# A decoder layer on one core: VectorE's part of the modulation as row sums over transposed weights, with one more quarter of the FFN's shift and scale given to VectorE

## The chip, the cores and the metric

The kernel runs on one core of a Trainium2 chip. The metric is the device time of one execution in microseconds. Three runs of the kernel before took 1273.33, 1273.87 and 1276.59 us; the median is 1273.87.

The engines are named as in the profile: TensorE (PE, with PEld for its weight loads), VectorE (DVE), ScalarE (ACT), GpSimd (POOL) and SyncE (SP), whose queue issues nearly all loads.

## The reference, cut to what matters

The layer takes 256 tokens of width 2048 in float32, and one conditioning vector c.

```
mod = silu(c) @ w_ada + b_ada                      # w_ada: 2048 x 12288
shift_a, scale_a, gate_a, shift_f, scale_f, gate_f = split(mod, 6)      # 2048 each
h = rms_norm(x, g_attn_pre) * (1 + scale_a) + shift_a
proj = h @ w_in                                    # 2048 x 5456
mixed = concat(diff_attention(proj), indexed_sparse_attention(proj)) @ w_o
x = x + gate_a * rms_norm(mixed, g_attn_post)
h = rms_norm(x, g_ffn_pre) * (1 + scale_f) + shift_f
ff = (silu(h @ w_gate) * (h @ w_up)) @ w_down      # inner width 5632
out = x + gate_f * rms_norm(ff, g_ffn_post)
```

The change concerns the first line alone: 2048 x 12288 products of a vector with a matrix, 96 MB of weights that are each read once.

## The kernel before, in words

**Large products.** Every weight block of 1 MB is loaded into one of five `raw` buffers (`RAW`), split exactly into two parts by ScalarE (`whi`, L168) and VectorE (`wlo`, L169), and multiplied in three matmuls of 128x512 (`mm3`, L178, L181, L182). The parts have three buffers each (`WB`).

**The order of the stages.** The projection `w_in` runs in five passes over groups of 1, 1, 2, 4 and 8 K tiles (`GROUPS`), so that the modulation of a later group can be made while an earlier one is multiplied. In the last pass the blocks of columns come in an order of their own, and after each block one step of attention work is taken (`attn_step`). Then come the output projection in two halves of its columns, with a step of attention after each block of the first half, and the feed-forward in three parts. Its first blocks run over half of the rows while the rest of the modulation is made.

**The modulation.** It is a list of units of 1 MB, in order of use (`units`). `ada_step` takes the next one; its load is issued up to two units ahead (`AHEAD`) into the same `raw` buffers, and a unit can end with a closing step (`finish`) that is taken with the next one. In the last projection pass one unit is taken with each block, or two with every fourth (`RATE`); in the output projection one with each block (`side`); in the first part of the feed-forward two (`FRATE`).

Two engines share the units. On TensorE (`on_pe`) a unit is four K tiles of 512 columns, each multiplied by a column of silu(c), and the four tiles go to four groups of columns of the array (L225). On VectorE a unit is four multiply-adds of 128x512 into `aacc` (L233): the weights times silu(c) as a column, with the sum over the partitions left to the end. There shift and scale close with small products with a column of ones (L286) on VectorE's side and with `sel` (L282) on TensorE's. A gate closes with a product with `ones` (L301) that leaves the same row on every partition.

- The attention's shift and scale are all on TensorE (`A_DVE` is empty).
- The attention's gate: blocks 0 and 1 on TensorE, 2 and 3 on VectorE (`GA_DVE`).
- The FFN's shift and scale: four quarters of eight units. Quarter 2 is on VectorE (`F_DVE`), the others on TensorE.
- The FFN's gate: all four blocks on VectorE, made during the feed-forward.

**Who sets the order.** The kernel is written against a planner (`schedule_with_timeline_sim=True`) that orders each engine's queue before the run by estimated times, with the written order as priority, and places waits and buffers. So instructions stand in the trace in another order than in the code. [...]

**Places.** `xx`, a 32 KB buffer per partition under the tag `bigB`, holds x and its transposed copy, later the attention's output (`mixT`) and the FFN's activations (`gT`). `late_rows` (L122) loads gains and biases as rows, and `to_cols` turns them into columns.

Of the kernel before, what the change touches and what calls it, by code (L numbers as in the profile page):

```python
# [24 lines left out]
T = 2  # L25
# [13 lines left out]
GROUPS = (1, 1, 2, 4, 8)  # L39
GA_DVE = (2, 3)  # L40
F_DVE = (2,)
A_DVE = ()
RATE = (1, 1, 1, 2)
ATT = 1
FRATE = 2
RAW = 5
# [10 lines left out]
def layer(ctx, tc, x, c, positions, w_ada, b_ada, g_attn_pre, g_attn_post, g_ffn_pre,  # L57
# [26 lines left out]
    # ---- constants  # L84
# [20 lines left out]
    # ---- vectors, brought to columns  # L105
# [6 lines left out]
    xx = big.tile([P, 2, 4096], F32, tag="bigB", name="xx")  # L112
    xs = xx[:, 0, :].rearrange("p (t d) -> p t d", t=T)
    xT = xx[:, 1, :].rearrange("p (k q) -> p k q", k=KT)
# [4 lines left out]
    R2 = wp.tile([49, P], F32, tag="hf", name="rows2", bufs=2)  # L119
# [64 lines left out]
    # ---- adaLN modulation  # L184
# [6 lines left out]
    def ada_block(col0s, n, on_pe, finish, brow=None):  # L191
# [8 lines left out]
        def new_acc(b):  # L200
            st["acc", b] = wp.tile([P, 512], F32, tag="aacc", name=nm("aacc"), bufs=2)

        def load(b, u):
            if u == 0 and brow is not None and (b == 0 or not on_pe):
                new_acc(b)
                if not on_pe:
                    POOL.memset(st["acc", b], 0.0)
                SP.dma_start(st["acc", b][0:1], brow)
            raw = wp.tile([P, 2048], F32, tag="raw", name=nm("raw"), bufs=RAW)
            st[b, u] = raw.rearrange("p (k n) -> p k n", n=n)  # L210
            SP.dma_start(st[b, u], ada_w[u * kk * P:(u + 1) * kk * P, col0s[b]:col0s[b] + n]  # L211
                         .rearrange("(k p) n -> p k n", p=P))

        def use(b, u):
            if u == 0 and b == 0 and on_pe:
                st["ps"] = adp.tile([P, 512], F32, tag="ad", name=nm("ad"))
            if u == 0 and brow is None and not on_pe:
                new_acc(b)
            for i in range(kk):
                k = u * kk + i  # L220
                w = st[b, u][:, i, :]
                if on_pe:
                    j = k % 4
                    extra = brow is not None and j == 0
                    PE.matmul(st["ps"][32 * j:32 * j + 32, :n], lhsT=c33[:, k, 1 - b:33 - b], rhs=w,  # L225
                              start=(b == 0 and k < 4), stop=(b == nb - 1 and k >= 12 and not extra),
                              tile_position=(0, 32 * j))
                    continue
                acc = st["acc", b][:, :n]
                if k == 0 and brow is None:  # L230
                    DVE.tensor_scalar(acc, w, csil[:, 0:1], None, op0=ALU.mult)
                else:
                    DVE.scalar_tensor_tensor(acc, w, csil[:, k:k + 1], acc, op0=ALU.mult, op1=ALU.add)  # L233
            if u == nu - 1 and b == nb - 1:
                if on_pe:
                    if brow is None:
                        new_acc(0)
                    acc = st["acc", 0]
                    if brow is not None:
                        PE.matmul(st["ps"][0:32, :n], lhsT=ident[0:1, 0:32], rhs=acc[0:1, :n],  # L240
                                  start=False, stop=True, tile_position=(0, 0))
                    ACT.activation(acc[:, :n], st["ps"][:, :n], AF.Copy)
                    after.append(lambda: finish([acc]))
                else:
                    after.append(lambda: finish([st["acc", b] for b in range(nb)]))
# [28 lines left out]
    # shift and scale as columns: shift, and gain*(1+scale)  # L274
    def ada_cols(dst, chunk, bcol, g, col, n, on_pe):
        m, k0 = n // P, col // P

        def finish(accs):
            ps = tr_bank()
            for i in range(m):  # L280
                if len(accs) == 1:
                    PE.matmul(ps[:, 2 * i:2 * i + 2], lhsT=accs[0][:, i * P:(i + 1) * P], rhs=sel,  # L282
                              start=True, stop=True)
                else:
                    for b in range(2):
                        PE.matmul(ps[:, 2 * i + b:2 * i + b + 1], lhsT=accs[b][:, i * P:(i + 1) * P],  # L286
                                  rhs=ones[:, 0:1], start=True, stop=True)
            d = dst[:, :, k0:k0 + m]
            DVE.tensor_tensor(d, ps[:, :2 * m].rearrange("p (m b) -> p b m", b=2),
                              bcol.rearrange("p (b k) -> p b k", b=2)[:, :, k0:k0 + m], op=ALU.add)  # L290
            DVE.scalar_tensor_tensor(d[:, 1], d[:, 1], 1.0, g[:, k0:k0 + m], op0=ALU.add, op1=ALU.mult)

        ada_block([chunk * D + col, (chunk + 1) * D + col], n, on_pe, finish)

    # gate times the post gain, the same row on every partition
    def ada_gate(G, chunk, col, on_pe):
        c0 = chunk * D + col

        def finish(accs):
            ps = tr_bank()  # L300
            PE.matmul(ps, lhsT=ones, rhs=accs[0], start=True, stop=True)  # L301
            DVE.tensor_tensor(G[:, col:col + 512], ps, G[:, col:col + 512], op=ALU.mult)

        ada_block([c0], 512, on_pe, finish, b_ada[0:1, c0:c0 + 512])

    # ---- first norm, transposed
    ssx = ct([P, T], "ssx")
    rx = ct([P, T], "rx")
    for t in range(T):
        ACT.activation(xx[:, 1, 2048 * t:2048 * t + 2048], xs[:, t], AF.Square, accum_out=ssx[:, t:t + 1])  # L310
# [11 lines left out]
    def make_h(H, src, mod, k, qs=slice(0, S), lk=None, on_act=True):  # L322
        """A K tile of gain*(1+scale)*x + shift, split in two; the work shared by ACT and DVE."""
# [18 lines left out]
    def group_h(gi, k0, nk):  # L342
        H = pp.tile([P, 2, max(GROUPS[gi % 2::2]), S], F32R, tag=f"h{gi % 2}", name=nm("h"))
        for k in range(nk):
            make_h(H, xT[:, k0 + k, :], modA, k0 + k, lk=k)
        Hs[gi] = H
# [21 lines left out]
    # ---- attention parts; keys of token tile 0: [0:128], of tile 1: [128:384]  # L368
# [19 lines left out]
    def to_T(dst_cols, copy_eng=None):  # L388
        """Transposes of [tokens, 128] column blocks, side by side in one bank."""
# [8 lines left out]
    def idx_pairs(p0):  # L398
        """Stages for the four indexer heads of two 128-column blocks."""
# [30 lines left out]
    def attn_step(admit=1):  # L430
        """Moves every job in flight by one stage, the oldest first, and admits new ones."""
# [552 lines left out]
```

## Time and profile before

| | before |
|---|---|
| median of three runs | 1273.87 us |
| span of the profiled execution | 1272.5 us |
| fastest run | 1273.33 us |
| TensorE busy | 1233.9 us (97%) |
| VectorE busy | 774.3 us (61%) |
| ScalarE busy | 560.9 us (44%) |
| mean DMA rate | 244 GB/s |
| mean granted TensorE clock | 0.993 |

The page gives the profiled execution by its span, from its first instruction to its last. The fastest run shown lies 0.8 us above that and the median 1.4 us. Busy times are sums over an engine's instructions; TensorE's matmuls overlap, so a busy share near 1 says that it rarely waits, not that each matmul is at its shortest.

### The profile page before, as it was taken

The numbers are of one execution on the slowest core, as the hardware profiler recorded it, in microseconds if no ns is written. First come the engines' busy times: TensorE is split into PE (matmuls) and PEld (weight loads), VectorE is DVE, ScalarE is ACT, GpSimd is POOL, SyncE is SP. The second block draws the span as 40 slices with busy tenths as digits, with TensorE's granted clock in tenths as the row PEclk, the third lists the DMA queues.
The fourth block names the chain that finished last, engine by engine and source line by source line (L and its number), as shares of the span: only waits on it lengthen the run. The fifth ranks groups of instructions, "written<-read, shape, count | busy, mean of one in ns | idle before, by whom it ended". The sixth has DMA issues, their size and how long they took to land.

```text
span 1272.5 us, 15272 instructions
## 1 busy us (share of the span) xinstructions
PE 1233.9 (97%) x5938; PEld 950.3 (75%) x5938; DVE 774.3 (61%) x1160; ACT 560.9 (44%) x806; POOL 21.4 (2%) x55
## 2 busy tenths in 40 slices
PE   4999999999999999899999999999999999999996
PEld 3666666777666786688887888888888888888885
DVE  3576455898598683758867545754455454445565
ACT  4733333345345543764444444444444334444442
POOL 1000000000000000200000000000000000000000
PEclk8999999999999999999999999999999999999998
DMA  9999997978687487858878656766556555565541
GB/s 307 339 343 327 347 381 278 314 263 321 211 285 268 142 329 289 306 167 286 282 264 290 200 193 222 251 227 198 176 189 199 190 188 190 194 198 182 184 164 66
DMA packets 160090, 310.13 MB, mean 244 GB/s; under 512 B 5785, under 2 KB 19978, under 8 KB 158738
## 3 DMA queue, kind: packets, MB, share of 16 engines
q1 hardware_dynamic: 159938, 309.14, 70.7%
q8 instruction: 46, 0.75, 0.2%
q14 instruction: 26, 0.21, 0.0%
q10 hardware_dynamic: 80, 0.02, 0.0%
HBM read 307.05 MB, written 2.10 MB: 243 GB/s over the span
## 4 chain that ended last, share of the span: by engine, by line
PE 88%; DMA 4%; DVE 4%; issue 1%; ACT 1%; SPq 1%; POOL 0%; DVEq 0%; POOLq 0%; ACTq 0%
PE mm L181 26%; PE mm L178 26%; PE mm L182 25%; PE ad L225 5%; DMA raw<-in_w_ada_dram 4%; DVE aacc L233 2%; DVE wlo L169 1%; PE tr L474 1%; PE tr L411 1%; PE tr L918 1%; PE tr L830 1%; SPq L211 1%; PE tr L392 1%; PE tr L301 0%; PE tr L282 0%
## 5 line engine op out<-in xcount | busy, mean ns | idle before, releaser
L169 DVE TENSOR_TENSOR wlo<-raw,whi 128x1024 fp32r<-128x1024 f32 (+1 forms) x383 | 462.3, 1212 | 338.6 <-ACT whi L168 337.7
L168 ACT ACTIVATE whi<-raw 128x1024 fp32r<-128x1024 f32 (+1 forms) x383 | 400.3, 1050 | 522.4 <-PE mm L182 458.1
L181 PE MATMUL mm<-wlo,h 128*128 128x512 f32 (+1 forms) x1056 | 416.8, 395 | 1.9 <-DVE wlo L169 1.9
L182 PE MATMUL mm<-whi,h 128*128 128x512 f32 (+1 forms) x1056 | 409.9, 389 | 0.2 <-DVE h L335 0.2
L178 PE MATMUL mm<-whi,h 128*128 128x512 f32 (+1 forms) x1056 | 381.4, 394 | 2.4 <-ACT h L330 1.4
L181 PEld LDWEIGHTS mm<-wlo,h 128*128 128x128 f32 x1056 | 198.9, 188 | 62.5 <-issue 9.5
L178 PEld LDWEIGHTS mm<-whi,h 128*128 128x128 f32 x1056 | 196.8, 188 | 63.2 <-issue 13.6
L182 PEld LDWEIGHTS mm<-whi,h 128*128 128x128 f32 x1056 | 198.3, 188 | 42.5 <-issue 3.0
L181 PE MATMUL mm<-wlo,gT 128*128 128x512 f32 x348 | 135.8, 390 | 0.0
L182 PE MATMUL mm<-whi,gT 128*128 128x512 f32 x348 | 135.4, 389 | 0.0
L178 PE MATMUL mm<-whi,gT 128*128 128x512 f32 x348 | 123.0, 390 | 0.0
L233 DVE SCALAR_TENSOR_TENSOR aacc<-raw,csil,aacc 128x512 f32<-128x512 f32 x126 | 94.1, 746 | 23.8 <-DMA raw<-in_w_ada_dram 22.5
L225 PE MATMUL ad<-raw,c 128*32 128x512 f32 (+2 forms) x640 | 79.6, 537 | 9.9 <-DMA raw<-in_w_ada_dram 9.9
L733 DVE TENSOR_TENSOR PR<-mm,PR 128x512 f32<-128x512 f32 (+1 forms) x88 | 57.1, 669 | 41.2 <-PE mm L182 41.0
L182 PEld LDWEIGHTS mm<-whi,gT 128*128 128x128 f32 x348 | 65.3, 188 | 13.8 <-issue 0.2
L181 PEld LDWEIGHTS mm<-wlo,gT 128*128 128x128 f32 x348 | 65.3, 188 | 13.7 <-issue 0.2
L178 PEld LDWEIGHTS mm<-whi,gT 128*128 128x128 f32 x348 | 65.3, 188 | 13.4
L181 PE MATMUL mm<-wlo,mixT 128*128 128x512 f32 x124 | 49.1, 397 | 0.0
L178 PE MATMUL mm<-whi,mixT 128*128 128x512 f32 x124 | 47.5, 400 | 0.6 <-ACT mixT L587 0.6
L182 PE MATMUL mm<-whi,mixT 128*128 128x512 f32 x124 | 46.4, 399 | 0.0
L225 PEld LDWEIGHTS ad<-raw,c 128*32 128x32 f32 x640 | 17.6, 116 | 36.4 <-issue 31.3
L181 PEld LDWEIGHTS mm<-wlo,mixT 128*128 128x128 f32 x124 | 23.3, 188 | 7.8 <-issue 2.5
(195 smaller groups left out, 678.8 us busy)
## 6 DMA issues: line engine op xcount, KB each, us to landing
raw<-in_w_ada_dram SPq DMA_DIRECT2D x96, 1024.0 KB, 7.1
raw<-in_w_gate_dram SPq DMA_DIRECT2D x44, 1024.0 KB, 5.2
raw<-in_w_up_dram SPq DMA_DIRECT2D x44, 1024.0 KB, 5.1
raw<-in_w_down_dram SPq DMA_DIRECT2D x44, 1024.0 KB, 5.2
raw<-in_w_in_dram SPq DMA_DIRECT2D x39, 1024.0 KB, 6.9
raw<-in_w_o_dram SPq DMA_DIRECT2D x16, 1024.0 KB, 5.0
xx<-in_x_dram SPq DMA_DIRECT2D x2, 1024.0 KB
x<-in_x_dram SPq DMA_DIRECT2D x2, 1024.0 KB, 4.7
```

Source lines behind the costliest of these rows:

```text
L168: ACT.activation(hv, src, AF.Copy)
L169: DVE.tensor_tensor(lv, src, hv.bitcast(F32), op=ALU.subtract)
L178: i = PE.matmul(ps, lhsT=hi, rhs=whi, start=start, stop=False)
L181: PE.matmul(ps, lhsT=hi, rhs=wlo, start=False, stop=False)
L182: PE.matmul(ps, lhsT=lo, rhs=whi, start=False, stop=stop)
L211: SP.dma_start(st[b, u], ada_w[u * kk * P:(u + 1) * kk * P, col0s[b]:col0s[b] + n] .rearrange("(k p) n -> p k n", p=P))
L225: PE.matmul(st["ps"][32 * j:32 * j + 32, :n], lhsT=c33[:, k, 1 - b:33 - b], rhs=w, start=(b == 0 and k < 4), stop=(b == nb - 1 and k >= 12 ...
L233: DVE.scalar_tensor_tensor(acc, w, csil[:, k:k + 1], acc, op0=ALU.mult, op1=ALU.add)
L392: PE.transpose(tr[:, i * P:(i + 1) * P], PR[:, t, c0:c0 + P], ident)
L411: PE.matmul(sc[i][:, SEG[t]], lhsT=st["q"][r, (2 * j + t) * P:(2 * j + t + 1) * P], rhs=ikT[r, :P * (t + 1)], start=True, stop=True)
L474: PE.matmul(sc[i][:, SEG[t]], lhsT=l, rhs=r, start=False, stop=(t == T - 1))
L733: DVE.tensor_tensor(dst, banks[c0][t][:, :n], dst, op=ALU.add)
```

## The change

A second copy of the modulation's weights, transposed (`w_adaT`, 12288 x 2048), is given to the kernel; the copy is made on the host. A unit on VectorE is then 128 rows of it, 128x2048, 8 KB of contiguous memory for each partition. One instruction multiplies it with silu(c), laid along the row on every partition (`csrow`), and sums along the row with the bias as the start. The result is a column, which is what shift and scale are kept as, so that they need no closing product. A gate needs a row, so `spread` makes a diagonal of four columns and multiplies it with `ones`. `spread` also makes `csrow`, in four pieces, behind the first group.

Quarter 1 of the FFN's shift and scale moves from TensorE to VectorE (`F_DVE`). The biases of the gates are loaded with the other rows (81 instead of 49), and no longer as rows of `aacc`. The 32 KB buffer becomes two of 16 KB (`Halves`), and one of the two buffers for `h` moves into the first. `if` for `elif` ahead of `group_h`, and an index by K tile in place of the group's, are the rest.

```diff
-F_DVE = (2,)
+F_DVE = (1, 2)
...
+        SP.dma_start(R2[49:65], b_rows[32:48])
+        SP.dma_start(R2[65:81], b_rows[80:96])
...
+    class Halves:
+        def __init__(self, name, nk):
+            self.parts = [big.tile([P, nk, S], F32R, tag=f"big{i}", name=nm(name)) for i in range(2)]
...
-                acc = st["acc", b][:, :n]
-                if k == 0 and brow is None:
-                    DVE.tensor_scalar(acc, w, csil[:, 0:1], None, op0=ALU.mult)
-                else:
-                    DVE.scalar_tensor_tensor(acc, w, csil[:, k:k + 1], acc, op0=ALU.mult, op1=ALU.add)
...
+    def ada_rows(col0, dst, bias, finish=None):
+        st = {}
+        def load():
+            st["raw"] = wp.tile([P, 2048], F32, tag="raw", name=nm("raw"), bufs=RAW)
+            SP.dma_start(st["raw"], w_adaT[col0:col0 + P])
+        def use():
+            DVE.tensor_tensor_reduce(out=st["raw"], in0=st["raw"], in1=csrow, scale=1.0, scalar=bias(),
+                                     op0=ALU.mult, op1=ALU.add, accum_out=dst())
+            if finish is not None:
+                after.append(finish)
+        units.append((load, use))
+
+    def spread(row, col):
+        m = wp.tile([P, 512], F32, tag="aacc", name=nm("dg"), bufs=2)
+        DVE.tensor_tensor(m.rearrange("p (k q) -> p k q", k=4),
+                          ident[:, None, :].to_broadcast([P, 4, P]),
+                          col[:, :, None].to_broadcast([P, 4, P]), op=ALU.mult)
+        ps = tr_bank()
+        PE.matmul(ps, lhsT=ones, rhs=m, start=True, stop=True)
+        if row is None:
+            return ps
+        ACT.activation(row, ps, AF.Copy)
...
+        for k in range(k0, k0 + m):
+            for b in range(2):
+                ada_rows((chunk + b) * D + k * P, lambda b=b, k=k: dst[:, b, k:k + 1],
+                         lambda b=b, k=k: bcol()[:, 16 * b + k:16 * b + k + 1],
+                         gain if (k, b) == (k0 + m - 1, 1) else None)
...
+        for i in range(4):
+            ada_rows(c0 + i * P, lambda i=i: part(i),
+                     lambda i=i: bcol[:, col // P + i:col // P + i + 1],
+                     (lambda: DVE.tensor_tensor(g, spread(None, st["g"]), g, op=ALU.mult))
+                     if i == 3 else None)
...
-        H = pp.tile([P, 2, max(GROUPS[gi % 2::2]), S], F32R, tag=f"h{gi % 2}", name=nm("h"))
+        if gi % 2:
+            H = big.tile([P, 2, 4, S], F32R, tag="big0", name=nm("h"))
+        else:
+            H = pp.tile([P, 2, 8, S], F32R, tag="h0", name=nm("h"))
...
+    csrow = ct([P, D], "csrow")
+    for a in range(0, KT, 4):
+        spread(csrow[:, a * P:(a + 4) * P], csil[:, a:a + 4])
...
-                elif bi == ns - 2:
+                if bi == ns - 2:
```

## Rows read from the trace of the kernel before

**Rows 1.** The page's busy times: us, share of the span, instructions.
```profile
PE 1233.9 (97%) x5938; PEld 950.3 (75%) x5938; DVE 774.3 (61%) x1160; ACT 560.9 (44%) x806; POOL 21.4 (2%) x55
```

**Rows 2.** The page's chain of waits, shares of the span by engine.
```profile
PE 88%; DMA 4%; DVE 4%; issue 1%; ACT 1%; SPq 1%; POOL 0%; DVEq 0%; POOLq 0%; ACTq 0%
```

**Rows 3.** What TensorE waited for: us in all, times, longest us.
```profile
PE ad L225 <- DMA raw<-in_w_ada_dram: 9.9, 2, 7.4
...
PE tr L830 <- POOL dg L848: 2.1, 1, 2.1
```

**Rows 4.** Windows: start:end, length, then each engine's busy us (instructions), clock, DMA share, GB/s.
```profile
240.00:300.00 60.00, 60.00 (x315) 44.72 (x313) 56.41 (x139) 30.07 (x70) 3.54 (x4) 1.00 0.87 308
355.00:450.00 95.00, 89.97 (x504) 64.88 (x501) 71.92 (x210) 48.43 (x127) 3.86 (x4) 1.00 0.70 243
396.00:430.00 34.00, 29.00 (x156) 21.73 (x155) 27.06 (x68) 17.54 (x54) 3.17 (x3) 1.00 0.61 214
450.00:500.00 50.00, 50.00 (x232) 38.48 (x232) 34.58 (x42) 19.87 (x25) 0.00 (x0) 1.00 0.84 305
```

**Rows 5.** Window of L225 alone, from 355 to 400 us.
```profile
355.00:400.00 45.00, 8.74 (x64) 1.77 (x64) 1.00 0.90 316
```

**Rows 6.** Window of L282 alone, from 400 to 512 us.
```profile
400.00:512.00 112.00, 1.01 (x8) 1.05 (x8) 1.00 0.70 249
```

**Rows 7.** Window of L286 alone, from 355 to 500 us.
```profile
355.00:500.00 145.00, 2.11 (x16) 2.71 (x16) 1.00 0.75 264
```

**Rows 8.** TensorE's groups by line and shape: count, busy us, mean ns, idle before.
```profile
L301 PE MATMUL tr<-aacc,ones 128*128 128x512 f32 x16 | 8.3, 598 | 0.0
```

**Rows 9.** VectorE's groups by line and shape.
```profile
L169 DVE TENSOR_TENSOR wlo<-raw,whi 128x1024 fp32r<-128x1024 f32 x374 | 455.4, 1223 | 334.9 <-ACT whi L168 334.0
L233 DVE SCALAR_TENSOR_TENSOR aacc<-raw,csil,aacc 128x512 f32<-128x512 f32 x126 | 94.1, 746 | 23.8 <-DMA raw<-in_w_ada_dram 22.5
...
L484 DVE TENSOR_REDUCE mx<-tr 128x1 f32<-128x256 f32 x24 | 9.9, 413 | 0.0
...
L484 DVE TENSOR_REDUCE mx<-tr 128x1 f32<-128x128 f32 x24 | 6.8, 284 | 4.7 <-PE tr L474 4.6
...
L843 DVE SCALAR_TENSOR_TENSOR x<-y,ry,x 128x1024 f32<-128x1024 f32 x4 | 5.0, 1281 | 1.8 <-POOL ry L145 1.8
...
L313 DVE TENSOR_SCALAR xx<-xx,rx 128x2048 f32<-128x2048 f32 x2 | 2.5, 1283 | 0.8 <-POOL rx L145 0.8
```

**Rows 10.** Windows of L233 alone.
```profile
355.00:450.00 95.00, 11.21 (x15) 1.00 0.70 243
450.00:500.00 50.00, 11.19 (x15) 1.00 0.84 305
```

**Rows 11.** VectorE's timeline around 415 us: start, us, instruction, idle before and releaser.
```profile
414.99 0.75 DVE L233 SCALAR_TENSOR_TENSOR aacc<-raw,csil,aacc 128x512 f32<-128x512 f32 x1 [1.60 <-DMA raw<-in_w_ada_dram]
415.66 0.17 DVE L516 RECIPROCAL l<-l 128x4 f32<-128x4 f32 x1
```

**Rows 12.** Timeline of the first 75 us.
```profile
8.37 0.20 ACT L138 ACTIVATE csil<-cols 128x16 f32<-128x16 f32 x1
...
12.76 1.93 PE L225 MATMUL ad<-raw,c 128*32 128x128 f32 x32 [7.42 <-DMA raw<-in_w_ada_dram]
...
27.57 1.50 PE L225 MATMUL ad<-raw,c 128*32 128x128 f32 x20 [2.52 <-DMA raw<-in_w_ada_dram]
```

**Rows 13.** SP's timeline, 5 to 40 us.
```profile
8.88 3.47 SPq L126 DMA_DIRECT2D pos_i<-in_positions_dram  x1
...
28.13 0.48 SPq L124 DMA_DIRECT2D rows<-in_b_ada_dram  x1
...
29.18 6.07 SPq L152 DMA_DIRECT2D raw<-in_w_in_dram  x2
```

**Rows 14.** The page's DMA issues: KB each, us to landing.
```profile
raw<-in_w_ada_dram SPq DMA_DIRECT2D x96, 1024.0 KB, 7.1
...
raw<-in_w_o_dram SPq DMA_DIRECT2D x16, 1024.0 KB, 5.0
```

More of the change, by code (lines that the diff above doesn't have):

```diff
@@ L56, in layer @@
 @with_exitstack
-def layer(ctx, tc, x, c, positions, w_ada, b_ada, g_attn_pre, g_attn_post, g_ffn_pre,
+def layer(ctx, tc, x, c, positions, w_ada, w_adaT, b_ada, g_attn_pre, g_attn_post, g_ffn_pre,
           g_ffn_post, w_in, lambda_q1, lambda_k1, lambda_q2, lambda_k2, g_diff_sub,
@@ L198, in ada_block, with new_acc @@
         nb = len(col0s)
-        def new_acc(b):
-            st["acc", b] = wp.tile([P, 512], F32, tag="aacc", name=nm("aacc"), bufs=2)
+        def new_acc():
+            st["acc"] = wp.tile([P, 512], F32, tag="aacc", name=nm("aacc"), bufs=2)
         def load(b, u):
[L204 to L208, printed above, removed]
+            if u == 0 and b == 0 and brow is not None:
+                new_acc()
+                SP.dma_start(st["acc"][0:1], brow)
             raw = wp.tile([P, 2048], F32, tag="raw", name=nm("raw"), bufs=RAW)
@@ L221, in use @@
                 w = st[b, u][:, i, :]
[L222 to L228, printed above, removed]
-                acc = st["acc", b][:, :n]
-                if k == 0 and brow is None:
-                    DVE.tensor_scalar(acc, w, csil[:, 0:1], None, op0=ALU.mult)
-                else:
-                    DVE.scalar_tensor_tensor(acc, w, csil[:, k:k + 1], acc, op0=ALU.mult, op1=ALU.add)
-            if u == nu - 1 and b == nb - 1:
[L235 to L245, printed above, removed]
+                j = k % 4
+                extra = brow is not None and j == 0
+                PE.matmul(st["ps"][32 * j:32 * j + 32, :n], lhsT=c33[:, k, 1 - b:33 - b], rhs=w,
+                          start=(b == 0 and k < 4), stop=(b == nb - 1 and k >= 12 and not extra),
+                          tile_position=(0, 32 * j))
+            if u == nu - 1 and b == nb - 1:
+                if brow is None:
+                    new_acc()
+                acc = st["acc"]
+                if brow is not None:
+                    PE.matmul(st["ps"][0:32, :n], lhsT=ident[0:1, 0:32], rhs=acc[0:1, :n],
+                              start=False, stop=True, tile_position=(0, 0))
+                ACT.activation(acc[:, :n], st["ps"][:, :n], AF.Copy)
+                after.append(lambda: finish(acc))
         for b in range(nb):
@@ L276, in ada_cols, with finish @@
         m, k0 = n // P, col // P
-        def finish(accs):
+        d = dst[:, :, k0:k0 + m]
+        def finish(acc):
             ps = tr_bank()
             for i in range(m):
[L281 to L288, printed above, removed]
-            DVE.tensor_tensor(d, ps[:, :2 * m].rearrange("p (m b) -> p b m", b=2),
-                              bcol.rearrange("p (b k) -> p b k", b=2)[:, :, k0:k0 + m], op=ALU.add)
-            DVE.scalar_tensor_tensor(d[:, 1], d[:, 1], 1.0, g[:, k0:k0 + m], op0=ALU.add, op1=ALU.mult)
@@ L293, in ada_cols @@
-        ada_block([chunk * D + col, (chunk + 1) * D + col], n, on_pe, finish)
-    def ada_gate(G, chunk, col, on_pe):
-        c0 = chunk * D + col
[L299 to L304, printed above, removed]
+                PE.matmul(ps[:, 2 * i:2 * i + 2], lhsT=acc[:, i * P:(i + 1) * P], rhs=sel,
+                          start=True, stop=True)
@@ new lines, in ada_gate, with finish, part @@
+    def ada_gate(G, chunk, col, on_pe, bcol):
+        c0 = chunk * D + col
+        g = G[:, col:col + 512]
+        if on_pe:
+            def finish(acc):
+                ps = tr_bank()
+                PE.matmul(ps, lhsT=ones, rhs=acc, start=True, stop=True)
+                DVE.tensor_tensor(g, ps, g, op=ALU.mult)
+            ada_block([c0], 512, finish, b_ada[0:1, c0:c0 + 512])
+            return
+        st = {}
+        def part(i):
+            if i == 0:
+                st["g"] = const.tile([P, 4], F32, tag="gcol", name=nm("gcol"), bufs=2)
+            return st["g"][:, i:i + 1]
+        for i in range(4):
[3 more added lines that the diff above has]
+                     if i == 3 else None)
@@ L691, in layer @@
     k0 = 0
-    for gi, nk in enumerate(sizes):
-        first, last = gi == 0, gi == len(sizes) - 1
+    for pi, nk in enumerate(sizes):
+        first, last = pi == 0, pi == len(sizes) - 1
         if last:
-            mixT[0] = big.tile([P, 2, KT, S], F32R, tag="bigB", name="mixT")
+            mixT[0] = Halves("mixT", KT)
             tc.keep_in_program_order(SP.dma_start(Ga, g_attn_post[0].partition_broadcast(P)))
-        if gi == 2:
+        if pi == 2:
             lamv = wp.tile([P, 4, 64], F32, tag="hf", name="lamv", bufs=2)
@@ L710, in layer @@
         if last:
-            spans = [(512 * ci, min(512, NPROJ - 512 * ci)) for ci in order]
+            spans = [(512 * ci, min(512, NPROJ - 512 * ci)) for ci in ORDER]
         blocks = [(si, a) for si in range(len(spans)) for a in range(k0, k0 + nk, 4)]
@@ L737, in layer @@
                 ada_step(RATE[bi % len(RATE)])
-                for _ in range(ATT):
-                    attn_step()
+                attn_step()
                 jobs.extend(newjobs)
@@ L790, in side @@
         ada_step(1)
-        for _ in range(ATT):
-            attn_step()
+        attn_step()
     def need_mix(ks):
```

56 lines of the change are left out of this document (31 added, 25 removed).

## The prediction

> **What bounds the kernel now.** I read the page's busy shares first: TensorE is busy 1233.9 of 1272.5 us, VectorE 774.3 [rows 1]. The reader should see an engine with 38.6 us idle in all and a second one, VectorE, at 61%. The chain of waits agrees, 88% of it is TensorE, 4% a DMA and 4% VectorE [rows 2]. TensorE's own list of waits names 9.9 us for the first modulation weights and then 2.1 us or less from any other line [rows 3]. So a microsecond taken off TensorE is worth a microsecond, as long as no other engine ends later in that stage. Which stage matters here I read from the windows [rows 4]: 355 to 450 us holds the end of the last projection pass, the first half of the output projection and most of the attention; TensorE is busy 89.97 of 95 us there and VectorE 71.92. All 5.0 us of idle lie in 396 to 430, where VectorE is at 27.06 of 34 (0.80). But in 240 to 300 VectorE ran 56.41 of 60 us (0.94) and TensorE did not idle at all. VectorE can therefore be loaded to 0.94 while TensorE runs on, and it can also hold TensorE up at 0.80: the forecast turns on which of the two the changed stretch resembles.
>
> **What leaves TensorE.** The second quarter of the FFN's shift and scale (call it F1; F0 to F3 are the four) is 8 units of 1 MB and 64 instructions, all between 355 and 400 us: 8.74 us [rows 5]. Its four closing products with `sel`, 8 instructions, go too: 1.01 us [rows 6]. F2, on VectorE before, loses its closing products with a column of ones: 16 instructions, 2.11 us [rows 7]. Sum 11.86 us, none of it beside other TensorE work. The gates' closing product with `ones` stays, through `spread`.
>
> **What comes to TensorE.** `csrow`, silu(c) as a row on every partition, takes four products of 128x512 with `ones`. The same product at L301 takes 16 instructions and 8.3 us for 8, so 1.04 us each and 4.1 us in all [rows 8]. silu(c) is there at 8.57 us, and TensorE waits 7.42 us up to 12.76 and 2.52 us up to 27.57 for weights [rows 12], so there is idle time that can hide them, if the planner puts them there. If it leaves them where they are written, behind the first group, they cost 4.1 us or a little more at a low clock. Bounds 0 and 4.1; I take 1.0, nearer to nothing because the planner already has the positions' load, written behind the first group too, at 8.88 [rows 13].
>
> **VectorE, unit by unit.** Before, a unit is four multiply-adds of 128x512 at 746 ns, 2.98 us [rows 9]. After, it is one multiply-and-sum of 128x2048, which the trace does not show. Nearest row: the multiply-add with two fp32 SBUF sources, 746 ns at 512 and 1281 ns at 1024 elements, so 1.045 ns per further element and 1281 + 1024 x 1.045 = 2.35 us. From below: a 128x2048 multiply by a column, 1.28 us. From above: a multiply pass and a sum pass apart, two of 1223 ns for the first and, by 284 ns at 128 and 413 ns at 256, 2.22 us for the second, 4.7 us. I take 2.35: the row has the same sources and type. A write of the sum may add a little; I leave it inside the range.
> [...]
> Count: before 126 multiply-adds, 94.1 us; after 40 units at 2.35, 94 us, and ten small diagonal products of 128x512 (four for `csrow`, one for each of six gate blocks) at 0.61 to 0.75 us, 7 us. VectorE's total hardly moves. Its place does: F1 adds 8 x 2.35 = 18.8 us into 355 to 450.
>
> **The stretch 355 to 450.** VectorE before: 71.92 us. The part of F2 in it, 15 of 30 multiply-adds and 11.21 us [rows 10], becomes 4 units, 9.4 us. With F1: 71.92 - 11.21 + 9.4 + 18.8 = 88.9 us. TensorE needs 95 - 8.74 - 1.01 = 85.3 us with its old idle time. At 0.94, 88.9 us of VectorE take 94.6 us: almost nothing would be gained here. But VectorE has 15 us free in 450 to 500 [rows 4], F2 there shrinks by another 1.8 us, and F1's results are wanted only when the output projection is done. How far can units lag? A unit's load is issued two units ahead of its use and five buffers are shared with the projection's own weights, so I let two units lag past 450: 88.9 - 4.7 = 84.2, over 0.94 = 89.6 us, a gain of 5.4. Bounds: 0.4 (none lags) and 9.75 (all of it hidden). F2's closing products, after 450, give their 2.11 in full since TensorE did not idle there.
>
> **Edits at nothing.** The split of the 32 KB buffer into two halves, `h1` moved into one of them, and the groups' new index: each new owner is first written well after the old one's last reader, in another stage for the attention output and the FFN's activations and a group later for `h`; if a group's `h` had to wait, it would be for products that TensorE is making anyway. The 81-row transposition instead of 49: one instruction. Two more small loads on SP's queue, 0.4 to 0.5 us each, in front of two loads of projection weights; those stand at 29.18 and the queue spent 6.07 us on them, most of it waiting for a buffer [rows 13], which covers it; without that 0.9 us. Six loads of bias rows and the POOL clears that SP waited for go: off the path. A unit's load now reads 8 KB rows instead of 2 KB ones; weights land 5.0 us after issue in w_o and 7.1 in w_ada [rows 14], so at most 2 us a unit either way, behind two units of lead. `if` for `elif` changes nothing, since the units of a group are always used by then. The gates on VectorE in 220 to 300 shrink by 8 x 0.63 = 5 us, less 1.4 for diagonals, and those in the FFN by 10 less 2.8, where TensorE did not idle: no gain.
>
> **Sum.** 5.4 + 2.1 - 1.0 = 6.5 us off. The profiled execution spans 1272.5 us, 1.4 below the median of the runs shown, and I take that difference along: span 1266.0, time 1273.87 - 6.5 = 1267.4 us.
>
> **Rivals.**
> Full gain: VectorE's surplus spreads to 500. There it has 106.5 - 22.4 + 16 x 2.35 = 121.7 us to do, 129.5 us at 0.94, and TensorE with its idle time 145 - 11.9 = 133.1: it fits. `csrow` hidden as well: 1262.0. For it: 240 to 300 us. Against: buffers are few and a unit stands ahead of its block's attention step in the planner's order.
> Slower, the attention chain: at 355 to 430 VectorE also carries top-k, softmax and the attention output's split, on which the output projection waits. Already now a multiply-add at 414.99 waits 1.60 us for its weights with a reciprocal of the softmax queued behind it [rows 11]. After the change twelve units instead of four stand there, each a block of 2.35 us, and 8.7 us less other work for TensorE to do meanwhile. If the stretch runs midway between 0.94 and 0.80, at 0.87: 88.9 / 0.87 = 102.2 us, +7.2, less 2.1, plus 1.0: 1280.0. It decides where VectorE's share stays under 88.9 / 96.1 = 0.925. Against: 0.80 holds in 34 of the 95 us only.
> Slower, a slow sum: 4.7 us a unit. In 355 to 500 VectorE has 84.1 + 75.2 = 159.3 us, at 0.94 169.5 against 145: +24.5; the gates before 300 us add some 4 and `csrow` 1: 1303. It turns to slower from about 3.2 us a unit, (144 x 0.94 - 84.1) / 16.
>
> **How the numbers follow.** Forecast 0.46 (its own range 1262 to 1273), full gain 0.16, attention chain 0.27, slow sum 0.11. Under 0.3%, about 3.8 us, a measurement of this kernel cannot tell from no change. Faster: all of the full gain and 0.34 of the forecast, 0.50. Same: 0.11 of the forecast and 0.12 of the chain, 0.23. Slower: the rest, 0.27. Range 1260 to 1285: it leaves out the slow sum, the best third of the full gain and the worst of the chain.
>
> **What would show it.** L225 with 64 instructions fewer; a row for the multiply-and-sum, x40, near 2.35 us (over 3.2 and I am wrong by the third rival); four products for `csrow` before 28 us; TensorE's idle time in the stretch between the last projection pass and the first half of the output projection still near 5 us, VectorE there above 0.9. Idle of 12 us or more there, released by VectorE or by the attention's ScalarE steps, is the second rival. I am also wrong if the gain shows in another stage, such as the start.

## The result: slower, 1305.5 us

The changed kernel takes 1305.53 us, the median of four runs (1303.36 to 1306.56), against 1274.51 for the kernel before in the same set. The ratio is 1.024, 95% interval 1.0224 to 1.0256. The forecast was 1267.4, and the range ended at 1285: the sign was wrong, and the time is some 20 us outside the range.

The page of the kernel after gives first the busy times and then the chain of waits by engine, as in [rows 1, 2].

```profile
PE 1246.8 (96%) x5858; PEld 955.9 (73%) x5858; DVE 784.8 (60%) x1120; ACT 563.3 (43%) x809; POOL 16.4 (1%) x49
...
PE 78%; DMA 8%; DVE 8%; issue 3%; ACT 2%; SPq 1%; POOL 0%; DVEq 0%; POOLq 0%; ACTq 0%
```

The span is 1304.7 us, so TensorE is idle for 57.9 us instead of 38.6, and although it has work taken away it is busy 12.9 us longer. VectorE's total rises by 10.5 us, and its share of the longer span is no larger; but its part in the chain has doubled from 4 to 8%. What TensorE waited for names the place:

```profile
PE tr L543 <- DVE s L609: 12.5, 2, 11.0
PE ad L230 <- DMA raw<-in_w_ada_dram: 10.4, 2, 7.4
...
PE tr L879 <- POOL dg L897: 3.0, 1, 3.0
PE tr L543 <- DVE s L567: 2.7, 2, 1.4
```

The first line is new: a transposition of the attention's weights `s` waits 11.0 us at a stretch for the difference of two heads on VectorE (L609). The windows are those of [rows 4].

```profile
240.00:300.00 60.00, 60.00 (x297) 43.34 (x298) 52.98 (x112) 25.82 (x52) 1.78 (x1) 1.00 0.98 354
355.00:450.00 95.00, 76.19 (x343) 53.68 (x342) 77.98 (x202) 38.36 (x102) 2.75 (x4) 0.82 0.58 205
396.00:430.00 34.00, 23.97 (x93) 16.21 (x93) 25.67 (x99) 10.50 (x40) 1.38 (x2) 0.59 0.31 103
450.00:500.00 50.00, 45.83 (x233) 36.01 (x232) 32.13 (x53) 23.61 (x47) 0.00 (x0) 1.00 0.66 234
```

In 355 to 450 TensorE is idle 18.8 us for 5.0 before, and the granted clock is 0.82 on average. In 240 to 300 it never idles, and executes 297 matmul instructions for 315. That is another mix of work: by the groups of this window 161 of them are large products of the projection (128x512) for 150 before, and 6 are products with the attention's transposed weights (`pT`) for 18. The attention is put off there, without any idle time. The next fence shows VectorE's groups for the sum, and TensorE's for the two products of the modulation that stay.

```profile
L257 DVE CUSTOM_DVE_ANT_0 raw<-raw,csrow,cols 128x2048 f32<-128x2048 f32 x40 | 93.8, 2346 | 29.7 <-DMA raw<-in_w_adaT_dram 29.7
...
L257 DVE DVE_READ_ACCUMULATOR2_ANT gcol<- 128x1 f32 x24 | 2.0, 82 | 0.0
```
```profile
L230 PE MATMUL ad<-raw,c 128*32 128x512 f32 x384 | 61.3, 604 | 0.0
L271 PE MATMUL tr<-dg,ones 128*128 128x512 f32 x20 | 10.1, 594 | 0.0
```

The sum takes 2346 ns, and 82 ns more to read it out: the estimate of 2.35 us a unit holds. L230 has its 64 instructions fewer. So a unit on VectorE costs what it was said to cost; most of the loss is in when it runs.

**The long wait, step by step.** VectorE's timeline in the kernel after, from 383 to 402 us (start, duration, line):

```profile
383.58 2.34 DVE L257 CUSTOM_DVE_ANT_0 raw<-raw,csrow,cols 128x2048 f32<-128x2048 f32 x1
...
388.19 0.61 DVE L532 TENSOR_REDUCE mx<-tr 128x1 f32<-128x128 f32 x2
...
389.93 2.34 DVE L257 CUSTOM_DVE_ANT_0 raw<-raw,csrow,cols 128x2048 f32<-128x2048 f32 x1
...
393.40 0.16 DVE L533 TENSOR_SCALAR mx<-mx 128x2 f32<-128x2 f32 x1
...
394.61 2.34 DVE L257 CUSTOM_DVE_ANT_0 raw<-raw,csrow,cols 128x2048 f32<-128x2048 f32 x1
...
397.74 0.17 DVE L605 RECIPROCAL rcp<-l 128x4 f32<-128x4 f32 x1
...
398.72 2.34 DVE L257 CUSTOM_DVE_ANT_0 raw<-raw,csrow,cols 128x2048 f32<-128x2048 f32 x1
...
401.39 0.73 DVE L609 SCALAR_TENSOR_TENSOR s<-s,w 128x128 f32<-128x128 f32 x2
```

The softmax is a string of short steps: the row maximum (L532), its sign (L533), the exponential on ScalarE, the reciprocal (L605), the difference (L609). From the maxima to the sign, to the reciprocal and to the difference, one whole sum stands in between each time: the three are 7.0 of the 12.6 us from the last maximum to the difference, and the rest are splits of weights and steps of the rotation and the top-k. VectorE is busy without a gap (from 380 to 412, in the next fence: 32.00 of 32 us). TensorE has nothing left to do by 390.9. These are the windows around it:

```profile
380.00:390.00 10.00, 10.00 (x54) 7.46 (x52) 10.00 (x21) 4.41 (x7) 0.00 (x0) 1.00 0.90 302
390.00:402.00 12.00, 0.98 (x5) 0.53 (x4) 12.00 (x28) 2.77 (x9) 0.00 (x0) 0.62 0.82 294
402.00:412.00 10.00, 7.78 (x31) 5.26 (x31) 10.00 (x44) 2.88 (x11) 0.00 (x0) 0.50 0.52 168
412.00:423.00 11.00, 9.36 (x29) 6.36 (x30) 7.28 (x31) 4.71 (x19) 0.88 (x2) 0.50 0.10 39
423.00:434.00 11.00, 10.47 (x52) 7.51 (x52) 4.59 (x16) 4.96 (x17) 1.18 (x2) 0.97 0.01 1
```

After the 11 us without work the granted clock is 0.50 up to 423, and what TensorE has then, mostly the attention's products, runs at it: 60 matmul instructions in 21 us.

### The profile page after: what moved, and what is told of

Same layout as the page of the kernel before. It is cut to its first block, busy times and chain, and to the rows that moved or that the text cites. A ratio compares the mean times of both kernels' runs of the same rounds, so it can differ in the third digit from the quotient of the medians.

```text
span 1304.7 us, 15036 instructions
## 1 busy us (share of the span) xinstructions
PE 1246.8 (96%) x5858; PEld 955.9 (73%) x5858; DVE 784.8 (60%) x1120; ACT 563.3 (43%) x809; POOL 16.4 (1%) x49
## 4 chain that ended last, share of the span: by engine, by line
PE 78%; DMA 8%; DVE 8%; issue 3%; ACT 2%; SPq 1%; POOL 0%; DVEq 0%; POOLq 0%; ACTq 0%
PE mm L191 23%; PE mm L188 23%; PE mm L192 22%; DMA raw<-in_w_adaT_dram 7%; PE ad L230 4%; DVE wlo L179 3%; DVE raw L257 2%; PE tr L522 1%; PE tr L459 1%; DMA rows<-in_b_ada_dram 1%; PE tr L879 1%; PE tr L967 1%; PE tr L271 1%; SPq L219 1%; DMA raw<-in_w_in_dram 0%
## 5 line engine op out<-in xcount | busy, mean ns | idle before, releaser
L257 DVE CUSTOM_DVE_ANT_0 raw<-raw,csrow,cols 128x2048 f32<-128x2048 f32 x40 | 93.8, 2346 | 29.7 <-DMA raw<-in_w_adaT_dram 29.7
L230 PE MATMUL ad<-raw,c 128*32 128x512 f32 (+2 forms) x576 | 75.0, 518 | 10.4 <-DMA raw<-in_w_ada_dram 10.4
L784 DVE TENSOR_TENSOR PR<-mm,PR 128x512 f32<-128x512 f32 (+1 forms) x88 | 57.9, 670 | 42.5 <-PE mm L192 41.8
L230 PEld LDWEIGHTS ad<-raw,c 128*32 128x32 f32 x576 | 15.9, 112 | 35.4 <-issue 30.4
L188 PEld LDWEIGHTS mm<-whi,mixT 128*128 128x128 f32 x124 | 23.7, 192 | 9.6 <-ACT mixT L581 2.6
```

The lines of the kernel that those rows point to most:

```text
L188: i = PE.matmul(ps, lhsT=hi, rhs=whi, start=start, stop=False)
L257: DVE.tensor_tensor_reduce(out=st["raw"], in0=st["raw"], in1=csrow, scale=1.0, scalar=bias(), op0=ALU.mult, op1=ALU.add, accum_out=dst())
L784: DVE.tensor_tensor(dst, banks[c0][t][:, :n], dst, op=ALU.add)
```

## The experiments

All times are medians; the ratio is to the kernel before, run on the same chip in the same set (1274.0 to 1274.7 us). The last two columns are read from the traces' timelines: the start of the first difference of two heads on VectorE, and of the last product of the output projection.

| run | time, us | ratio (95% interval) | first difference | last product of w_o |
|---|---|---|---|---|
| before | 1274.5 | | 248.4 | 511.3 |
| after | 1305.5 | 1.024 (1.0224 to 1.0256) | 265.1 | 541.5 |
| e1_undo_move | 1302.1 | 1.0215 (1.02 to 1.023) | 265.4 | 538.1 |
| e2_move_alone | 1291.5 | 1.0132 (1.0117 to 1.0147) | 247.1 | 527.9 |
| e3_last_quarter | 1301.8 | 1.0216 (1.0199 to 1.0233) | 265.9 | 532.0 |
| e4_attention_first | 1306.5 | 1.0251 (1.0236 to 1.0266) | 269.6 | 542.1 |
| e5_cut4 | 1309.3 | 1.0275 (1.0259 to 1.0291) | 259.4 | 529.7 |
| e6_csrow_load | 1291.0 | 1.0131 (1.0115 to 1.0147) | 251.8 | 527.6 |
| e7_layout_only | 1274.6 | 1.0006 (0.9997 to 1.0016) | 247.2 | 510.7 |
| e8_old_gate | 1288.7 | 1.0116 (1.01 to 1.0132) | 255.1 | 527.1 |
| e9_cut4_wide | 1287.4 | 1.0103 (1.0087 to 1.012) | 257.5 | 525.7 |
| e10_load_and_gate | 1281.5 | 1.0064 (1.0047 to 1.0081) | 248.4 | 519.9 |
| e11_load_gate_move | 1296.0 | 1.0169 (1.0147 to 1.0192) | 249.7 | 531.2 |
| e12_load_gate_cut | 1277.7 | 1.0028 (1.0017 to 1.0039) | 248.4 | 515.3 |
| e13_ffn_gate_only | 1279.4 | 1.0042 (1.0029 to 1.0054) | 247.9 | 515.7 |
| e14_none_on_vectore | 1277.6 | 1.0027 (1.0014 to 1.004) | 247.0 | 514.6 |

### First set: is it the quarter that moved, or the rest?

Theory Q was that the moved quarter F1 lengthens VectorE's queue in 355 to 450; theory F that the form of the sums costs the time, with or without F1.

**e1_undo_move**: the changed kernel, F1 back on TensorE.

```diff
-F_DVE = (1, 2)
+F_DVE = (2,)
```

> The kernel after with one line undone: quarter 1 of the FFN's shift and scale is back on TensorE, all else stays transposed. Theory Q (the queue: F1's eight sums stand in VectorE's queue ahead of the attention's work in a stretch that has no room for 19 us more, so attention comes late to the output projection): most of the 31 us comes back, 1275 to 1286 us, and the wait of TensorE on the softmax product in the output projection falls from 11 us to under 3. Rival F (the form: 2.35 us blocks in place of four of 0.75, and the row of silu(c), delay attention from the gates on): 1290 us or more, the softmax product of the first head still some 15 us later than before. Rival S (the price of the start): 6 us of the loss sit before the last projection pass and stay under every theory.

1302.1: only 3.4 us less. The long wait is gone (the longest for L609 is 2.3 us), the attention is as late as before the edit (265.4), and the end hardly moves. Q alone falls.

The 27 us that are left are mostly not idle time: TensorE is busy 1252.6 us in e1 for 1233.9 before, and idle 46.8 for 38.6. The same 640 instructions of the modulation (L230) take 7.6 us longer (the last section has why), the products for `csrow` 4.0. The mean clock of 0.93 in the window below, which holds the attention's end, costs some 6 us, an estimate from 0.07 of 95 us.

```profile
355.00:450.00 95.00, 87.32 (x429) 55.63 (x428) 69.27 (x194) 41.51 (x108) 2.76 (x4) 0.93 0.64 221
```

**e2_move_alone**: the kernel before, with the old multiply-adds, and F1 on VectorE.

```diff
-F_DVE = (2,)
+F_DVE = (1, 2)
```

> The kernel before with F1 alone moved to VectorE, in the old form of multiply-adds (8 x 2.98 us = 24 us instead of 19). Theory Q: slower than before by at least 15 us, 1290 to 1312, since the place is the trouble and the old form is longer. Rival F: about as before or a little faster, 1264 to 1278, since the small pieces let the attention's work in between.

1291.5: the move alone costs 16.8 us, on a kernel whose attention starts on time, as Q has it. So both are costly, and they don't add: 16.8 for the move and 27.4 for the rest (1302.1 - 1274.7) are 31 together. On an attention that is late already, F1 costs only 3.4 us more (e1 to the kernel after).

**e3_last_quarter**: F3, made later, moved in place of F1.

```diff
-F_DVE = (1, 2)
+F_DVE = (2, 3)
```

> The kernel after with quarter 3 instead of quarter 1 on VectorE: the same work is taken off TensorE, but its eight sums fall behind the attention, where VectorE was at 3 to 5 tenths before (480 to 510 us). Theory Q: 1266 to 1280 us, at or under the kernel with the move undone, and no wait of 11 us. Rival F: 1290 us or more, like the kernel after less a few us.

1301.8, the same as with no move (e1), as F has it. The last product of w_o comes 6.1 us sooner than in e1, and is paid back at once: in 510 to 540 TensorE is busy 22.2 of 30 us (30.0 in e1) and VectorE 25.8 (14.7). Off the attention, a moved quarter is worth nothing here, and costs nothing.

**e4_attention_first**: in the written order, each step of attention ahead of its unit; the same swap stands in the output projection.

```diff
-                ada_step(RATE[bi % len(RATE)])
                 attn_step()
...
+                ada_step(RATE[bi % len(RATE)])
```

> The kernel after with the two lines swapped that take a unit of the modulation and a step of attention in each block, so that attention is written first and has the planner's priority. Theory Q: the attention chain is late because units stand in front of it, so 1275 to 1292 us, top-k done well before the 416 us of the kernel after. If VectorE's sheer load in the stretch is the trouble and not the order in its queue, 1300 to 1310, no change beyond 5 us. Rival F: no change beyond 5 us either.

1306.5, no better, with the first difference 4 us later still. The written order is not the lever.

### Second set: which part of the rest?

Three theories: G, the grain (a sum of 2.35 us can't be passed); L, the places of the buffers; S, the later start, 183.4 us for 177.6 at the last step of the attention's shift and scale, after four products for `csrow`:

```profile
36.76 1.92 PE L271 MATMUL tr<-dg,ones 128*128 128x512 f32 x4
...
41.25 1.02 PE L271 MATMUL tr<-dg,ones 128*128 128x512 f32 x2
...
42.80 1.02 PE L271 MATMUL tr<-dg,ones 128*128 128x512 f32 x2
```

These eight instructions are 3.96 us of TensorE, in a stretch where it does not wait.

**e5_cut4**: e1 with each sum in four pieces.

```diff
-            DVE.tensor_tensor_reduce(out=st["raw"], in0=st["raw"], in1=csrow, scale=1.0, scalar=bias(),
-                                     op0=ALU.mult, op1=ALU.add, accum_out=dst())
+            part_ = wp.tile([P, 4], F32, tag="cutc", name=nm("cutc"), bufs=4)
+            for i in range(4):
...
+                                         in1=csrow[:, 512 * i:512 * i + 512], scale=1.0,
+                                         scalar=bias() if i == 0 else part_[:, i - 1:i],
+                                         op0=ALU.mult, op1=ALU.add,
+                                         accum_out=dst() if i == 3 else part_[:, i:i + 1])
```

> The changed kernel with F1 back on TensorE (1302.1 us), and each sum of 128x2048 cut into four of 128x512, each starting from the one before; nothing else. VectorE then has more to do, not less: a piece should take about 0.75 us and 0.08 us for reading its sum, so 3.3 us a unit for 2.43. Theory G (grain): one instruction of 2.35 us can't be passed by the small steps of the attention that come up while it runs, and in 220 to 300 us the first difference of two heads comes at 265 us for 248 before; cut into pieces as long as the old multiply-adds, the attention should come most of the way back: 1280 to 1294. Theory L (the places of the buffers) and theory S (the start: four products for csrow, TensorE 6 us late at 184 us) expect no gain, and with 0.9 us more a unit rather a loss: 1300 to 1308.

1309.3, against G. But the marks say otherwise: the attention came 6 us earlier and w_o ended 8.4 us earlier. The loss lies in the feed-forward, where a stretch with no idle and full clock had 1306 matmuls in 300 us for 1336 in e1. That was taken up again as e9.

**e6_csrow_load**: e1 with `csrow` from a load of c and one silu, ahead of the last pass.

```diff
-    for a in range(0, KT, 4):
-        spread(csrow[:, a * P:(a + 4) * P], csil[:, a:a + 4])
...
+            SP.dma_start(csrow, c[0].partition_broadcast(P))
+            ACT.activation(csrow, csrow, AF.Silu)
```

> The changed kernel with F1 back on TensorE, and csrow made from a load of c to every partition and one silu on ScalarE, before the last projection pass, in place of four diagonals, four products of 128x512 and four copies near the start. Theory S: the start's delay is what makes the attention late, so about all of the 27 us over the kernel before comes back: 1275 to 1285. Theory G: only the start's own 4 to 6 us comes back: 1295 to 1299. Theory L: the same as G here.

1291.0, between the two: 11.1 us back for a start that is 7.7 us earlier (176.0 for 183.7), with the first difference 13.6 us earlier. The products for `csrow` are 4.0 us of the start's delay. Most of the rest are the modulation's products of 128x256 behind them, which the other order breaks up; e1, then e6, which has the 4.1 us of the kernel before:

```profile
L230 PE MATMUL ad<-raw,c 128*32 128x256 f32 x64 | 7.6, 389 | 0.0
```
```profile
L230 PE MATMUL ad<-raw,c 128*32 128x256 f32 x64 | 4.1, 384 | 0.0
```

On its way the delay grows here; through which steps was not followed.

**e7_layout_only**: the kernel before with the new places alone.

```diff
-    xx = big.tile([P, 2, 4096], F32, tag="bigB", name="xx")
+    xs = big.tile([P, T, D], F32, tag="big0", name="xs")
+    xT = big.tile([P, KT, S], F32, tag="big1", name="xT")
```

> The kernel before with the new places alone (two buffers of 16 KB for the one of 32 KB, the second h in the first of them, the index by K tile), the old multiply-adds, no csrow, F1 on TensorE. Theory L: the places cost the time: 1290 to 1302. Theories G and S: nothing in it is late: 1271 to 1278.

1274.6, the kernel before. L is out for these places; the 8 KB of `csrow` are not in this run.

**e8_old_gate**: e1 with the attention's gate in the old form.

```diff
-        ada_gate(Ga, 2, b * 512, b not in GA_DVE, bGa)
+        (old_gate(Ga, 2, b * 512, False) if b in GA_DVE else ada_gate(Ga, 2, b * 512, True, bGa))
```

> The changed kernel with F1 back on TensorE and the attention's gate (blocks 2 and 3, 8 units in 220 to 300 us) made by the old multiply-adds; F2 and the FFN's gate stay sums, csrow stays. Theory G: the attention is no later than the start makes it, the first difference of two heads within 8 us of the 248 before: 1276 to 1290. Theories L and S: 1298 to 1304, as with the sums.

1288.7: 13.5 us back from eight units, with the first difference at 255.1 us, as G has it. The old form also loads other blocks and closes otherwise; that the length of a sum counts by itself is for the next set. S is left for the rest.

### Third set: the cut again, and both together

**e9_cut4_wide**: e5, with 512 bytes for the part sums.

```diff
-            part_ = wp.tile([P, 4], F32, tag="cutc", name=nm("cutc"), bufs=4)
+            part_ = wp.tile([P, 128], F32, tag="cutc", name=nm("cutc"), bufs=4)
```

> The same as the sums cut in four (1309.3 us), but the four part sums lie in a buffer of 512 bytes per partition in place of 16 bytes, so that the buffers behind it stand at other places by multiples of 512. With 16 bytes the large products of the feed-forward came every 232 ns at full granted clock, for 227 in the other kernels, and the time from the first product with gT to the end was 577 us for 564. Theory P (place): the 16 bytes moved TensorE's operands to places that it reads more slowly; at 512 the 227 ns come back, and 1309.3 less about 13 in the feed-forward and up to 6 ahead of it: 1290 to 1297, which is below the kernel with whole sums (1302.1), as theory G (grain) wants it. Theory W (the pieces' work itself slows TensorE, by 128 accumulator reads and instructions): 1306 to 1311.

1287.4: 14.7 us less than whole sums (e1), although VectorE has 0.9 us more to do for each of 32 units, and below the 1290 to 1297 of theory P. The gain stands ahead of the feed-forward: from the last product of w_o to the end of the span it is 761.9 us in e9 and 761.3 in e1 (778.5 in e5). So it is not VectorE's total but the whole sum as one piece, with the order that the planner makes for it. The first softmax shows where the time goes, in VectorE's timelines: before, then after, then e9.

```profile
242.91 1.14 DVE L484 TENSOR_REDUCE mx<-tr 128x1 f32<-128x128 f32 x4
...
248.44 0.74 DVE L561 SCALAR_TENSOR_TENSOR s<-s,w 128x128 f32<-128x128 f32 x2
```
```profile
251.74 0.61 DVE L532 TENSOR_REDUCE mx<-tr 128x1 f32<-128x128 f32 x2
...
253.04 2.34 DVE L257 CUSTOM_DVE_ANT_0 raw<-raw,csrow,cols 128x2048 f32<-128x2048 f32 x1
...
256.08 0.16 DVE L533 TENSOR_SCALAR mx<-mx 128x2 f32<-128x2 f32 x1
...
259.02 0.17 DVE L605 RECIPROCAL rcp<-l 128x4 f32<-128x4 f32 x1
259.11 2.32 DVE L257 CUSTOM_DVE_ANT_0 raw<-raw,csrow,cols 128x2048 f32<-128x2048 f32 x1
...
262.19 0.21 DVE L607 SCALAR_TENSOR_TENSOR w<-l,nlam,rcp 128x2 f32<-128x2 f32 x1
...
265.12 0.74 DVE L609 SCALAR_TENSOR_TENSOR s<-s,w 128x128 f32<-128x128 f32 x2
```
```profile
249.50 1.14 DVE L537 TENSOR_REDUCE mx<-tr 128x1 f32<-128x128 f32 x4
...
257.51 0.74 DVE L614 SCALAR_TENSOR_TENSOR s<-s,w 128x128 f32<-128x128 f32 x2
```

From the end of these maxima to the difference it is 4.4 us before, 12.8 after and 6.9 with pieces. The queue's order is the planner's. Of the 12.8 us two whole sums are 4.7 and splits `wlo` of the projection's weights 6.5; before, five multiply-adds of 0.74 us and one split stand there. How much the length of a sum does by itself, and how much the other order that the planner makes with it, the runs don't separate. TensorE doesn't idle meanwhile: it makes the projection's products first, and the attention's are left for later.

**e10_load_and_gate** has the edits of e6 and e8 together.

> The two edits that gave 11 and 13 us back, together: csrow from a load of c, and the attention's gate by the old multiply-adds; F1 on TensorE, F2 and the FFN's gate as sums. If the two are apart (the start's delay, and VectorE's long instructions among the attention's first steps): 1302.1 - 11.1 - 13.5 = 1277.5, so 1273 to 1282, which leaves 0 to 8 us over the kernel before for F2's sums in the output projection. If both take the same microseconds: 1286 to 1290. If F2's lost closing products (2.1 us) are all that is left of the change's gain: 1271 to 1274.

1281.5, 4 us above the 1277.5 of the sum and just inside its range: 20.6 of 24.6 us, mostly apart.

**e11_load_gate_move** is e10 with F1 on VectorE (`F_DVE = (1, 2)`).

> The same with F1 on VectorE as well, as sums. Theory A (VectorE's load in 355 to 450 makes the attention's end late, as when F1 moved alone: +17 us): 1286 to 1300. Theory N (F1 costs only behind an attention that is late already): within 5 us of the run without the move, or below it by up to 10: 1264 to 1282.

1296.0: F1 costs 14.5 us on an attention that is on time, theory A. The window 360 to 400 of e11, and its longest wait of TensorE:

```profile
360.00:400.00 40.00, 27.90 (x128) 21.05 (x129) 39.50 (x95) 14.48 (x29) 0.00 (x0) 0.81 0.90 316
```
```profile
PE tr L613 <- DVE s L679: 12.7, 3, 9.5
```

VectorE is at 39.5 of 40, and TensorE loses 12.1 us (0.14 us in e10).

### Fourth set: what is left, and the other direction

**e12_load_gate_cut** is e10 with the sums that are left cut as in e9.

> The run with csrow loaded and the attention's gate in the old form (1281.5 us), with the sums that are left (F2's 8 units in the output projection, the FFN gate's 16) cut in four, the part sums in 512 bytes. If F2's whole sums in the output projection are what is left of the loss (7.5 us over the kernel before), they lose it as the gate's did: 1271 to 1276. If it is the load of csrow or something else that the cut doesn't touch: 1279 to 1285, the pieces' 0.9 us a unit included.

**e13_ffn_gate_only** is e10 with F2 in the old form; only the feed-forward's gate is sums.

> The same with F2 in the old form altogether (multiply-adds, closing products with a column of ones), so that only the feed-forward's gate is made of whole sums, 16 units at a place without attention. If F2's sums are what is left: 1272 to 1277, at the kernel before. If the load of csrow (1 MB written and one silu on ScalarE ahead of the last pass) costs it: 1279 to 1285. If whole sums in the feed-forward cost: between the two.

e12 took 1277.7 and e13 1279.4. The first falls between its cases, the second on the lower edge of the case for the load. Cutting the sums of F2 and of the FFN's gate gives 3.8 us, F2 in the old form 2.1, and some 4 to 5 us over the kernel before stay in both. The load of `csrow` is in both, and part of the rest is its silu. In e12 it holds ScalarE up, the splits behind it come late, and TensorE waits for one of them:

```profile
187.65 1.28 ACT L822 ACT_TABLE_LOAD   x1
188.94 1.92 ACT L822 ACTIVATE csrow<-csrow 128x2048 f32<-128x2048 f32 x1
```
```profile
195.00 0.50 PE L191 MATMUL mm<-wlo,h 128*128 128x512 f32 x1 [1.27 <-DVE wlo L179]
```

From 176 to 300 us TensorE waits 2.2 us in all in e12 and in e13, and never in the kernel before. Where the other 2 or 3 us come from was not shown. No version of these beats the kernel before.

**e14_none_on_vectore** is the kernel before with no quarter on VectorE.

```diff
-F_DVE = (2,)
+F_DVE = ()
```

> The other direction: the kernel before with F2 back on TensorE too (no quarter of the FFN's shift and scale on VectorE). TensorE gets 8.7 us of products and 1 us less of closing products. Theory A (VectorE's load between 355 and 500 us sets how late the attention ends, and a late attention costs TensorE its idle time and clock): the attention ends earlier and part of the 7.6 us is paid back, 1274 to 1280. If the price of F1 on VectorE (+17 us) were the same in both directions per quarter: 1262 to 1268. If VectorE is not the limit before the change: 1281 to 1284.

1277.6: TensorE gets 7.6 us of work net (8.7 and 1.0 for F2's share, less 2.1 for its old closing products) and the time rises by 3.6, as A has it. In 355 to 450 its idle time falls from 5.0 us to 1.9:

```profile
355.00:405.00 50.00, 50.00 (x280) 30.57 (x278) 36.42 (x124) 22.17 (x59) 1.38 (x2) 1.00 0.88 312
405.00:450.00 45.00, 43.06 (x258) 32.01 (x258) 25.27 (x64) 24.63 (x66) 1.38 (x2) 1.00 0.59 194
```

So of the three shares tried with the old multiply-adds the one before is the best: one quarter fewer costs 3.6 us, one more 16.8.

## Why the prediction was wrong

**Right.** The unit: 2.35 us forecast, 2.346 measured, with 0.08 for the read-out. The third rival (a slow sum) is out: from 512 columns (748 ns, e5) to 2048 (2346 ns) the sum takes 1.04 ns per further element, as in [rows 9]. L225's 64 instructions and L286 are gone. The edits that move buffers cost nothing (e7). The mechanism of the second rival, VectorE's share under 0.925 in 355 to 450 and the softmax's chain late, is what F1 does: the share is 77.98 of 95, 0.82, and TensorE's 18.8 us of idle time pass the 12 that were named as this rival's sign.

One reading was off without bearing on the sum: TensorE's list of waits has, behind the 9.9 us, 5.0 us for the rows of biases at the start (L130), and not "2.1 us or less from any other line".

**Wrong, the step that decided: "The stretch 355 to 450".** It read from 240 to 300 us that VectorE "can therefore be loaded to 0.94 while TensorE runs on", and let units lag. That window had products of the projection for TensorE to do meanwhile; after 377 us, when the last of them is added to PR in the kernel after, TensorE has the output projection, which waits for the attention, and the attention itself. VectorE did reach 0.97 in 360 to 400 (38.67 of 40 us), and TensorE stood still because of it. F1 costs 16.8 us by itself (e2) and 14.5 (e11), where the forecast had a gain of 5.4 and the rival a loss of 7.2, 6.1 over all. Under-priced was what follows the wait: the granted clock of 0.50 from 402 to 423.

**Wrong, the step with no rival: "The gates on VectorE in 220 to 300 shrink ... no gain".** The total shrank, and the time rose. Eight whole sums there cost 13.5 us (e1 to e8), and 14.7 us come back by cutting all sums, though that lengthens the total (e1 to e9). The step counted microseconds on an engine that was off the bound, and not how long the next short step of a chain is kept waiting: by instructions of 2.35 us for 0.75, and by the order that the planner makes with them (4.4 us from the maxima to the first difference became 12.8).

**Mis-sized: `csrow`.** Taken at 1.0 with an upper bound of 4.1; the products take 3.96 with nothing to hide them, since the planner left them where they are written, and they break up the units behind them (7.6 us for 4.1). The load in their place gives 11.1 us beside the gate's whole sums (e1 to e6) and 7.2 without them (e8 to e10), for a start that is 7.7 and 7.6 us earlier: the delay grows only in the first case.

**Mis-sized: the 8.74 us that leave TensorE.** L230 falls from 79.6 to 75.0 us, 4.5 for 64 instructions less: the 576 that stay were 70.8 us before. The reason stands below.

Together the parts are 14.5 to 16.8 (F1), 9.5 to 13.5 (the gate's sums, e6 to e10 and e1 to e8), 7.2 to 11.1 (the start), 2 to 4 (F2's sums, with the cut of the FFN gate's in the 4) and 4 or 5 that e12 and e13 leave, of which some 2 are seen as waits; they overlap, and 31 is what is seen.

## What to carry to other kernels

A long instruction was priced here by what stood behind it in its engine's queue: where a chain of short steps passed through VectorE, four pieces of 0.75 us beat one of 2.35, even at a higher total (1287.4 us in e9 for 1302.1 in e1, with another order from the planner). A share of busy time that did no harm in one stage said nothing of another (0.94 in 240 to 300 us before, 0.97 in 360 to 400 after); look at what the bound engine has to do meanwhile, and at how its clock stands after a wait (0.50 from 402 to 423 us here). And a delay at the start isn't a constant: nearly the same one was worth 7 or 11 us at the end, by what it met.

## What the runs showed of the hardware

**The size of a small buffer changed TensorE's pace by some 2%.** e5 and e9 differ only in a buffer of 16 or 512 bytes per partition for the part sums, which lets the buffers behind it stand at other places. These are the large products of the feed-forward from 800 to 1000 us, e5 and then e9:

```profile
L191 PE MATMUL mm<-wlo,h 128*128 128x512 f32 x251 | 99.4, 396 | 0.0
```
```profile
L191 PE MATMUL mm<-wlo,h 128*128 128x512 f32 x256 | 100.0, 391 | 0.0
```

Near 1100 us they follow each other by some 0.231 us in e5 and 0.227 in e9, and in 700 to 1000 us there are 1306 of all matmul instructions in e5 and 1341 in e9, both without idle and at full granted clock. It is not the work of the pieces: the last starts at 845.1 us in e5, and in 1100 to 1200 it is still 440 for 451. In all it is 22 us (1309.3 and 1287.4), 17 of them behind the last product of w_o. That the places of TensorE's operands are the reason is inferred from the edit, not shown, and which operand's it would be was not tried.

**One narrow product took as long as four.** A product here is two instructions, as in [rows 8], whose 16 instructions are 8 products, so a unit of four K tiles is eight. TensorE's timeline of the kernel after, both near 100 us:

```profile
99.47 1.06 PE L230 MATMUL ad<-raw,c 128*32 128x512 f32 x8
...
104.43 1.04 PE L230 MATMUL ad<-raw,c 128*32 128x512 f32 x2
```

The eight instructions of a whole unit overlap: 1.06 us in all, where one has a mean of 604 ns. Two by themselves take as long, 1.04 us. So units that the new order breaks up cost more on TensorE: in e1 the same 640 instructions as before are 87.2 us, for 79.6.
